# Further rows' products of an expert in three groups instead of six, with two transpositions and some conversions moved

## The chip, the cores and the metric

One core of a Trainium2 chip runs the whole kernel. The metric is the device time of one execution in microseconds, the median of several runs. TensorE multiplies, VectorE and ScalarE work on what it leaves in PSUM and on data in SBUF, GpSimd (POOL) gathers and scatters rows, SyncE (SP) issues most loads.

## What is computed

A hybrid encoder layer over 1024 positions of width 1024: a mixer (short convolution and a Fourier group), cross-attention to 256 memory tokens, and a mixture of experts. All that the change touches is in the last part:

```python
logits = (hf @ w_router).astype(jnp.float32) + b_router.astype(jnp.float32)
top_v, top_i = lax.top_k(logits, TOP_K)          # 4 of 32 experts for each position
...
gu = xb @ w_gate_up[e] + b_gate_up[e]
gate = jnp.minimum(gu[:, :D_EXPERT], SWIGLU_LIMIT)
up = jnp.clip(gu[:, D_EXPERT:], -SWIGLU_LIMIT, SWIGLU_LIMIT)
glu = gate * jax.nn.sigmoid(SWIGLU_ALPHA * gate)
return ((up + 1.0) * glu) @ w_down[e] + b_down[e]
```

Each expert has 1024 x 2048 weights for gate and up, and 1024 x 1024 for down, all fp32.

## The kernel before

**Records and chunks.** An expert works on a block of 128 gathered rows, its main rows. Experts with more rows than that get a second, smaller set, the further rows (rem in the code): 32 records for the 17 best-filled experts after the first one, 64 for the first (STATIC), none for the other 14. Experts stand in an order in which those with further rows (heavy) and those without (light) mostly alternate; expert 8 is heavy, between two light ones. An expert's weights are twelve chunks of 1 MB: 0 to 7 are gate and up (0 to 3 give the first half of the hidden width, g0 and u0, 4 to 7 the second, g1 and u1), 8 to 11 are down.

**Main products.** Weights and rows are split into a high part and a rest, so that three products in the faster fp32r form (`eh`, `el` of a chunk with the high part and the rest of the rows; lines 1072 to 1074) stand for one in fp32. `main_mm` issues twelve products a chunk. The split of a chunk, here called its conversion, is a ScalarE copy (`eh<-raw`, line 135) and a VectorE subtraction (`el<-raw,eh`, line 136).

**Further products.** `rem_mm` (line 1095) multiplies the further rows by the raw chunk in plain fp32. With 32 records a product needs 32 columns of the array, and four products (two halves of the contraction, two chunks) run side by side in four column strips. One call takes two chunks, eight products; six calls serve an expert. The sums of two calls share a bank: r0 (chunks 0 to 3), r1 (4 to 7), rd (8 to 11). The trace books each of these products twice, so eight show as x16. `take_rem` copies a bank out on ScalarE (`re<-r`, line 1113), `h_rem` transposes it, adds the bias and does its SwiGLU; `y_rem` finishes rd.

**Places.** The code writes its own order (manual schedule): each engine runs its instructions as they are written. An expert has 24 places, two a chunk: place 2j is in the middle of chunk j's products, 2j + 1 behind them. `PLACE_...` give the places of four transpositions for each kind of expert: the two halves of hh, the main rows' SwiGLU result (`h_main`: transposed on TensorE, line 1019, then split on both engines as `hthl`), and two for the next expert's rows (`x_main`, `xthl`). SwiGLU itself (`swiglu`, lines 1011 to 1014) is emitted at places 7 and 15, on VectorE and with one sigmoid on ScalarE. `REM` gives, in `plan`, the places of the further rows' steps relative to the expert: `lead` for the products, `lx` for `x_rem` (the further rows' own transposition, line 1045).

**Room.** Raw chunks and converted pairs live in one set of 18 slots. `load_more` issues a load, and `split_to` a conversion, at each place as far as a table (`AHEAD_...`) allows and there is room; a raw chunk's slot is free when its conversion and, in a heavy expert, the further product that reads it are written (`used_raw`). So when further products are written later, later conversions and loads follow.

Of the kernel before, what the change touches and what calls it, by code (L numbers as in the profile page):

```python
# [47 lines left out]
AHEAD_REM = (2, 3, 4, 5)  # L48
AHEAD_LOOP = (1, 5, 5, 6, 5, 5, 4, 5, 5, 7, 6, 7, 6, 4, 3, 6, 5, 6, 5, 6, 4, 5, 6, 5)
AHEAD_LAST = (1, 4, 3, 5, 4, 4, 3, 2, 2, 5, 4, 5, 4, 4, 3, 4, 3, 4, 3, 5, 4, 5, 4, 5)  # L50
REM = (2, 4, 0, 4, 4, 1)
PLACE_HEAVY = (13, 17, 19, 21)
PLACE_LIGHT = (13, 18, 20, 21)
PLACE_FIRST = (10, 17, 18, 21)
PLACE_LOOP = (13, 17, 21, 23)
PLACE_LAST = (11, 16, 0, 0)
KINDS = ("first", "heavy", "light", "loop", "last")
AHEAD = dict(zip(KINDS, (AHEAD_FIRST, AHEAD_HEAVY, AHEAD_LIGHT, AHEAD_LOOP, AHEAD_LAST)))
PLACE = dict(zip(KINDS, (PLACE_FIRST, PLACE_HEAVY, PLACE_LIGHT, PLACE_LOOP, PLACE_LAST)))

# [20 lines left out]
def kernel(ctx: ExitStack, tc: tile.TileContext, A, out, dbg=None):  # L81
    nc = tc.nc
# [10 lines left out]
    def mm_bank(name="mm"):  # L93
        return mmp.tile([P, H2], F32, name=name, tag="mm")

    def tp_bank(name="tp"):
        return tpp.tile([P, H2], F32, name=name, tag="tp")

    def sm_bank(name="sm"):
        return smp.tile([P, H2], F32, name=name, tag="sm")  # L100
# [4 lines left out]
    def s4(name, shape, dt=F32):  # L105
        return mp.tile(list(shape), dt, name=name, tag="s4", bufs=7)

    def t2(name, shape=(P, H2), dt=F32):
        return mp.tile(list(shape), dt, name=name, tag="t2", bufs=6)
# [8 lines left out]
    def f(ap):  # L118
        return ap.bitcast(F32)
# [459 lines left out]
    ps = {}  # L579
# [39 lines left out]
    for ft in range(KT):  # L619
        wh, wl = next_w(0)  # L620
        for h in range(2):
            xr = t2("xres")
            nc.sync.dma_start(out=xr, in_=A["xT"][h, ft])
            for g, (yh, yl) in enumerate(((ych, ycl), (yfh, yfl))):
                ps = mm_bank()
# [15 lines left out]
            q = t2("sq") if ft else row4[h]  # L641
# [102 lines left out]
    for fc in range(2):  # L744
        VW.append([(s8(f"vwh{fc}{q}", [P, 4, H2], F32R), s8(f"vwl{fc}{q}", [P, 4, H2], F32R)) for q in range(2)])
        for hd in range(4):
            w = next_w(0)
            for mt in range(2):
                ps = mm_bank()
# [3 lines left out]
                j = hd * 2 + mt  # L753
# [169 lines left out]
    ch = {}  # L923
# [18 lines left out]
    def scatter_add(dst, idx, src):  # L942
        nc.gpsimd.indirect_dma_start(out=dst, out_offset=bass.IndirectOffsetOnAxis(ap=idx, axis=0),  # L943
                                     in_=src, in_offset=None, compute_op=ALU.add)
# [35 lines left out]
    def whole(q):  # L980

        return q < WHOLE_FIRST or q >= NE * 12 - WHOLE_LAST

    def used_raw(q):
        ch[q][3] -= 1
        dead[0] += ch[q][3] == 0

    def split_to(n):
        while nsplit[0] < min(n, nload[0]):
            q = nsplit[0]  # L990
            c = ch[q]
            if not whole(q):
                if room() < 2:
                    return
                pairs[0] += 1
                c[1], c[2] = s8("eh", [P, 4, H2], F32R), s8("el", [P, 4, H2], F32R)
                split(c[0], c[1], c[2])
                used_raw(q)
            nsplit[0] += 1
# [9 lines left out]
    def swiglu(dst, g, u1, sg, u):  # L1009

        nc.scalar.activation(sg, g, AF.Sigmoid, scale=ALPHA)  # L1011
        nc.vector.tensor_scalar(u, u1, LIMIT + 1.0, 1.0 - LIMIT, op0=ALU.min, op1=ALU.max)
        nc.vector.scalar_tensor_tensor(u, sg, SIGMOID_LIMIT, u, op0=ALU.min, op1=ALU.mult)  # L1013
        nc.vector.scalar_tensor_tensor(dst, g, LIMIT, u, op0=ALU.min, op1=ALU.mult)  # L1014
# [62 lines left out]
            if k == 1 and middle:  # L1077
                middle()

    def rem_mm(i, j):  # L1080

        s = st[i]
        m = s["m"]
        c, g = (j // 4, (j % 4) // 2) if j < 8 else (0, (j - 8) // 2)
        lhs = s["xr"] if j < 8 else s["hr"]
        key = "r" + (str(c) if j < 8 else "d")
        n = 64 // m
        if g == 0:
            s[key] = sm_bank(key)
        ps = s[key]  # L1090
        for k in range(4 // n):
            for u in range(n):
                for t in range(2):
                    kk, o = u * 2 + k, (u * 2 + t) * m
                    nc.tensor.matmul(ps[o:o + m], lhs[:, g * 4 + kk, :], ch[12 * i + j - 1 + t][0][:, kk, :],  # L1095
                                     start=k == 0 and g == 0, stop=k == 4 // n - 1 and g == 1)
        for q in (j - 1, j):
            used_raw(12 * i + q)

    def glu_main(i, c):  # L1100
        s = st[i]
        s[f"h{c}"] = t2("hh")
        swiglu(s[f"h{c}"], s[f"g{c}"], s[f"u{c}"], t2("sg"), t2("u"))
# [7 lines left out]
    def take_rem(i, c):  # L1111
        r = st[i][f"re{c}"] = t2("re")
        nc.scalar.activation(r, st[i][f"r{c}"], AF.Copy)

    def h_rem(i, c):

        s = st[i]
        m = s["m"]
        if c == 0:
            s["hr"] = s4("hrt", [P, KT, m])  # L1120
        tb = tp_bank()
        for j in range(4):
            nc.tensor.transpose(tb[:, j * P:(j + 1) * P], s[f"re{c}"][:, j * P:(j + 1) * P], ident)
        tv = s[f"re{c}"][:, :8 * m].rearrange("p (j t n) -> p j t n", j=4, t=2)
        tw = tb.rearrange("p (j u t n) -> p j u t n", j=4, u=64 // m, t=2)
        nc.vector.tensor_tensor(tv, tw[:, :, 0], s["bT"][:, c, :, :, None].to_broadcast([P, 4, 2, m]), op=ALU.add)
        if m == 32:
            nc.vector.tensor_tensor(tv, tv, tw[:, :, 1], op=ALU.add)  # L1128
        ab = t2("ga").rearrange("p (a j n) -> p a j n", a=2, j=4)
        a, b = ab[:, 0, :, :m], ab[:, 1, :, :m]  # L1130
        swiglu(s["hr"][:, c * 4:c * 4 + 4, :], tv[:, :, 0], tv[:, :, 1], a, b)
# [8 lines left out]
    def y_rem(i):  # L1140
        s = st[i]
        m, rd = s["m"], s["rd"]
        n = 2 * m
        yr, w = t2("yr"), f(s["idr"][:n, 1:2])
        if m == 32:
            nc.scalar.activation(yr[:n], rd[n:], AF.Copy)
            nc.vector.tensor_tensor(yr[:n], rd[:n], yr[:n], op=ALU.add)
            nc.scalar.activation(yr[:n], yr[:n], AF.Copy, scale=w)
        else:
            nc.scalar.activation(yr, rd, AF.Copy, scale=w)  # L1150
        scatter_add(acc_d.rearrange("r (b w) -> (r b) w", w=H2), s["ids"][:n], yr[:n])

    def expert(i, hook=None, last=False):

        s = st[i]
        m, postponed = s["m"], s["r"] == STATIC
        n = i + 1 if i + 1 < NE else None
        kind = "first" if i == 0 else "last" if i == NE - 1 else "loop" if i == NE - 2 else "heavy" if m else "light"
        h0, h1, x0, x1 = PLACE[kind]
        ahead = AHEAD[kind]  # L1160
        todo = {p: [] for p in range(24)}
        todo[7].append(lambda: glu_main(i, 0))
        todo[15].append(lambda: glu_main(i, 1))

        def rem_postponed():
            x_rem(i)
            for p in (1, 3, 5, 7):
                rem_mm(i, p)
                if p % 4 == 3:
                    take_rem(i, p // 4)  # L1170
                load_more(eng=nc.gpsimd)
                split_to(12 * i + 7 + AHEAD_REM[p // 2])
            h_rem(i, 0)

        todo[h0].append(lambda: h_main(i, 0))
        todo[h1].append(lambda: h_main(i, 1))
        if n:
            todo[x0].append(lambda: x_main(n, 0))
            todo[x1].append(lambda: x_main(n, 1))
        if postponed:  # L1180
            todo[15].append(rem_postponed)
            todo[19] += [lambda: rem_mm(i, 9), lambda: h_rem(i, 1)]
            todo[23] += [lambda: rem_mm(i, 11), lambda: y_rem(i)]

        def place(p):
            for t in todo[p] + agenda.pop(24 * i + p, []):
                t()
            if p == 23 and not last:
                y_main(i)
            load_more(eng=nc.gpsimd if i == 0 else nc.sync)  # L1190
            split_to(12 * i + p // 2 + ahead[p])

        for j in range(12):
            load_more(eng=nc.gpsimd if i == 0 else nc.sync)
            if hook and j in hook:
                hook[j]()
            q = 12 * i + j
            main_mm(i, (0, 1, 2, 3, 4, 5, 6, 7, 8, 10, 9, 11)[j] if last else j, lambda: place(2 * j))
            if whole(q):
                used_raw(q)  # L1200
            else:
                pairs[0] -= 1
            place(2 * j + 1)

    def plan(i):

        lead, lx, lt, l0, l1, ly = REM
        at = lambda p, fn, *arg: agenda.setdefault(p, []).append(lambda: fn(*arg))
        p = 24 * i - 2 * lead + 1
        at(p + 2 - lx, x_rem, i)  # L1210
        for j in range(1, 12, 2):
            at(p + 2 * j, rem_mm, i, j)
        for c, l in ((0, l0), (1, l1)):
            at(p + 8 * c + 6 + lt, take_rem, i, c)
            at(p + 8 * c + 6 + l, h_rem, i, c)
        at(p + 22 + ly, y_rem, i)
# [309 lines left out]
    base, r = fin["base"], fin["r"]  # L1526
# [89 lines left out]
```

## Time and profile before

| | |
|---|---|
| median of 3 runs | 2056.21 us (2055.64 to 2057.71) |
| the profiled execution's own time | 2057.09 us |
| its span, first to last instruction | 2054.5 us |
| TensorE busy | 2014.3 us, 98% of the span |
| VectorE busy | 1546.7 us, 75% |
| ScalarE busy | 1117.8 us, 54% |
| main products of the experts (1072 to 1074) | 992 and 496 of each line, 390 to 415 ns booked for one |
| further products (1095) | x1152 r, 601 ns booked for one |

The experts begin near 600 us and fill the rest. Times of a product are booked durations; products overlap, so the distance from start to start is what counts for the end. Idle time of an engine stands in brackets, with what ended it.

### The profile page before, as it was taken

To read this page: it belongs to the slowest core of one execution; us is meant where nothing else is said; L and a number is where in the kernel's file an instruction comes from. 1 tells how busy PE (TensorE), PEld (TensorE's weight loads), DVE (VectorE), ACT (ScalarE), POOL (GpSimd) and SP (SyncE) were. 2 spreads that over 40 slices of the span, in tenths; PEclk is the share of its full clock that TensorE was granted. 3 is DMA by queue.
4 is the path that set the end of the run, shared out by engine and by line. 5 is a ranking of instruction groups with operands and counts; after the bars stand their busy time and mean duration, and the time that the engine had idled before them with its cause. 6 is when DMAs were issued, how large, how long until landed. Compare 5 with 4: busy or idle time off the path is not lost. (4 is left out here: it accounts for less than half of the span.)

```text
span 2054.5 us, 28594 instructions
## 1 busy us (share of the span) xinstructions
PE 2014.3 (98%) x10745; PEld 1522.1 (74%) x10745; DVE 1546.7 (75%) x1914; ACT 1117.8 (54%) x1195; POOL 238.4 (12%) x190
## 2 busy tenths in 40 slices
PE   8999999999988999999999999999999999999997
PEld 6888988888983567677776677776777676776764
DVE  6667768446575677888878788878888778888776
ACT  5233533334222565676656576666766566666664
POOL 0000100000133011021111111111111110110111
PEclk9999999999999999999999999999999999999998
DMA  4122434112358689898897888898998798898986
GB/s 157 47 62 72 124 129 158 42 41 91 106 190 291 222 288 362 298 326 329 308 360 279 308 322 324 311 374 285 330 327 308 280 372 300 322 332 305 354 290 265
DMA packets 104638, 513.25 MB, mean 250 GB/s; under 512 B 21297, under 2 KB 25650, under 8 KB 55346
## 3 DMA queue, kind: packets, MB, share of 16 engines
q1 hardware_dynamic: 83600, 445.87, 57.6%
q0 software_dynamic: 14080, 48.54, 9.5%
q10 hardware_dynamic: 6818, 16.99, 2.4%
q8 instruction: 85, 1.39, 0.3%
q14 instruction: 55, 0.45, 0.1%
HBM read 473.41 MB, written 37.95 MB: 249 GB/s over the span
## 5 line engine op out<-in xcount | busy, mean ns | idle before, releaser
L136 DVE TENSOR_TENSOR el<-raw,eh 128x2048 fp32r<-128x2048 f32 x372 | 831.6, 2286 | 125.5 <-ACT eh L135 125.5
L135 ACT ACTIVATE eh<-raw 128x2048 fp32r<-128x2048 f32 x372 | 692.5, 1910 | 28.7 <-PE g L1074 23.9
L1072 PE MATMUL g<-eh,xthl 128*128 128x512 f32 x992 | 393.7, 397 | 0.0
L1074 PE MATMUL g<-eh,xthl 128*128 128x512 f32 x992 | 386.7, 390 | 2.1 <-issue 2.1
L1073 PE MATMUL g<-el,xthl 128*128 128x512 f32 x992 | 387.6, 391 | 0.0
L1072 PEld LDWEIGHTS g<-eh,xthl 128*128 128x128 f32 x992 | 186.2, 188 | 66.6 <-issue 27.7
L1074 PEld LDWEIGHTS g<-eh,xthl 128*128 128x128 f32 x992 | 186.3, 188 | 42.7 <-issue 2.6
L1073 PEld LDWEIGHTS g<-el,xthl 128*128 128x128 f32 x992 | 186.4, 188 | 37.2
L1072 PE MATMUL d<-eh,hthl 128*128 128x512 f32 x496 | 205.9, 415 | 0.0
L1074 PE MATMUL d<-eh,hthl 128*128 128x512 f32 x496 | 195.1, 393 | 0.0
L1073 PE MATMUL d<-el,hthl 128*128 128x512 f32 x496 | 194.0, 391 | 0.0
L1095 PE MATMUL r<-raw,xrt 128*32 128x512 f32 (+1 forms) x1152 | 146.5, 601 | 0.7 <-ACT xrt L1046 0.7
L135 ACT ACTIVATE hthl<-tp 128x512 fp32r<-128x512 f32 x62 | 37.1, 599 | 163.0 <-PE tp L1019 163.0
L943 POOL DMA_INDIRECT acc_d<-y,idx x31 | 75.3, 2431 | 387.3 <-ACT y L1137 292.7
L1072 PEld LDWEIGHTS d<-eh,hthl 128*128 128x128 f32 x496 | 93.2, 188 | 28.0 <-ACT xthl L135 10.9
L1011 ACT ACTIVATE ga<-re 128x128 f32<-128x128 f32 (+1 forms) x36 | 11.4, 316 | 186.6 <-DVE re L1128 180.1
L1074 PEld LDWEIGHTS d<-eh,hthl 128*128 128x128 f32 x496 | 93.1, 188 | 21.2
L1073 PEld LDWEIGHTS d<-el,hthl 128*128 128x128 f32 x496 | 93.6, 189 | 16.0
L146 PE MATMUL mm<-xh,wh 128*128 128x512 f32 x232 | 92.2, 397 | 5.9 <-ACT xh L138 5.9
L939 POOL DMA_INDIRECT xg<-h_d,idx x32 | 55.2, 1726 | 359.1 <-DMA idx<-tab_d 242.0
L148 PE MATMUL mm<-xh,wl 128*128 128x512 f32 x232 | 91.0, 392 | 0.5 <-DVE wl L136 0.5
L147 PE MATMUL mm<-xl,wh 128*128 128x512 f32 x232 | 91.0, 392 | 0.0
(378 smaller groups left out, 3256.2 us busy)
## 6 DMA issues: line engine op xcount, KB each, us to landing
raw<-in_w_exp SPq DMA_DIRECT2D x375, 1024.0 KB, 7.7
raw<-in_w_exp POOLq DMA_DIRECT2D x9, 1024.0 KB, 13.3
wraw<-in_w_in SPq DMA_DIRECT2D x15, 512.0 KB, 5.1
xraw<-in_xT SPq DMA_DIRECT2D x16, 256.0 KB, 6.1
wraw<-in_w_k SPq DMA_DIRECT2D x8, 512.0 KB, 3.6
wraw<-in_w_v SPq DMA_DIRECT2D x8, 512.0 KB, 3.6
wraw<-in_w_out SPq DMA_DIRECT2D x8, 512.0 KB, 3.9
xres<-in_xT SPq DMA_DIRECT2D x16, 256.0 KB, 2.7
```

The costliest lines, as they stand in the source:

```text
L135: nc.scalar.activation(dh, src, AF.Copy)
L136: nc.vector.tensor_tensor(dl, src, f(dh), op=ALU.subtract)
L146: nc.tensor.matmul(ps, lh, rh, start=start and i == 0, stop=False)
L147: nc.tensor.matmul(ps, lh, rl, start=False, stop=False)
L148: nc.tensor.matmul(ps, ll, rh, start=False, stop=stop and i == n - 1)
L939: nc.gpsimd.indirect_dma_start(out=dst[:m], out_offset=None, in_=src[:, :], in_offset=bass.IndirectOffsetOnAxis(ap=idx[:m, 0:1], axis=0))
L943: nc.gpsimd.indirect_dma_start(out=dst, out_offset=bass.IndirectOffsetOnAxis(ap=idx, axis=0), in_=src, in_offset=None, compute_op=ALU.add)
L1011: nc.scalar.activation(sg, g, AF.Sigmoid, scale=ALPHA)
L1072: nc.tensor.matmul(ps, l[:, 0, kk, :], wh[:, k, :], start=j >= 8 and g == 0 and k == 0, stop=False)
L1073: nc.tensor.matmul(ps, l[:, 0, kk, :], wl[:, k, :], start=False, stop=False)
L1074: nc.tensor.matmul(ps, l[:, 1, kk, :], wh[:, k, :], start=False, stop=g == 1 and k == 3)
L1095: nc.tensor.matmul(ps[o:o + m], lhs[:, g * 4 + kk, :], ch[12 * i + j - 1 + t][0][:, kk, :], start=k == 0 and g == 0, stop=k == 4 // n - 1 ...
```

## The change

Three edits. `rem_mm` takes a list of halves: by default it does both calls of a bank in one go, sixteen products, so r0, r1 and rd are each one group; `plan` calls it for j = 3, 7 and 11, where formerly the second call of each bank stood. The first expert (STATIC) keeps its calls one by one. `REM` moves `x_rem` four places, two chunks, later. `PLACE_HEAVY` and `PLACE_LOOP` move the transposition of hh's first half from place 13 to 12.

```diff
--- before.py
+++ after.py
@@ -48,11 +48,11 @@
 AHEAD_REM = (2, 3, 4, 5)
 AHEAD_LOOP = (1, 5, 5, 6, 5, 5, 4, 5, 5, 7, 6, 7, 6, 4, 3, 6, 5, 6, 5, 6, 4, 5, 6, 5)
 AHEAD_LAST = (1, 4, 3, 5, 4, 4, 3, 2, 2, 5, 4, 5, 4, 4, 3, 4, 3, 4, 3, 5, 4, 5, 4, 5)
-REM = (2, 4, 0, 4, 4, 1)
-PLACE_HEAVY = (13, 17, 19, 21)
+REM = (2, 0, 0, 4, 4, 1)
+PLACE_HEAVY = (12, 17, 19, 21)
 PLACE_LIGHT = (13, 18, 20, 21)
 PLACE_FIRST = (10, 17, 18, 21)
-PLACE_LOOP = (13, 17, 21, 23)
+PLACE_LOOP = (12, 17, 21, 23)
 PLACE_LAST = (11, 16, 0, 0)
 KINDS = ("first", "heavy", "light", "loop", "last")
 AHEAD = dict(zip(KINDS, (AHEAD_FIRST, AHEAD_HEAVY, AHEAD_LIGHT, AHEAD_LOOP, AHEAD_LAST)))
@@ -1077,25 +1077,27 @@
             if k == 1 and middle:
                 middle()
 
-    def rem_mm(i, j):
+    def rem_mm(i, j, gs=(0, 1)):
 
         s = st[i]
         m = s["m"]
-        c, g = (j // 4, (j % 4) // 2) if j < 8 else (0, (j - 8) // 2)
+        j -= j % 4
         lhs = s["xr"] if j < 8 else s["hr"]
-        key = "r" + (str(c) if j < 8 else "d")
+        key = "r" + (str(j // 4) if j < 8 else "d")
         n = 64 // m
-        if g == 0:
+        if 0 in gs:
             s[key] = sm_bank(key)
         ps = s[key]
-        for k in range(4 // n):
-            for u in range(n):
-                for t in range(2):
-                    kk, o = u * 2 + k, (u * 2 + t) * m
-                    nc.tensor.matmul(ps[o:o + m], lhs[:, g * 4 + kk, :], ch[12 * i + j - 1 + t][0][:, kk, :],
-                                     start=k == 0 and g == 0, stop=k == 4 // n - 1 and g == 1)
-        for q in (j - 1, j):
-            used_raw(12 * i + q)
+        for g in gs:
+            for k in range(4 // n):
+                for u in range(n):
+                    for t in range(2):
+                        kk, o = u * 2 + k, (u * 2 + t) * m
+                        nc.tensor.matmul(ps[o:o + m], lhs[:, g * 4 + kk, :], ch[12 * i + j + 2 * g + t][0][:, kk, :],
+                                         start=k == 0 and g == 0, stop=k == 4 // n - 1 and g == 1)
+        for g in gs:
+            for t in range(2):
+                used_raw(12 * i + j + 2 * g + t)
 
     def glu_main(i, c):
         s = st[i]
@@ -1165,7 +1167,7 @@
         def rem_postponed():
             x_rem(i)
             for p in (1, 3, 5, 7):
-                rem_mm(i, p)
+                rem_mm(i, p, (p % 4 // 2,))
                 if p % 4 == 3:
                     take_rem(i, p // 4)
                 load_more(eng=nc.gpsimd)
@@ -1179,8 +1181,8 @@
             todo[x1].append(lambda: x_main(n, 1))
         if postponed:
             todo[15].append(rem_postponed)
-            todo[19] += [lambda: rem_mm(i, 9), lambda: h_rem(i, 1)]
-            todo[23] += [lambda: rem_mm(i, 11), lambda: y_rem(i)]
+            todo[19] += [lambda: rem_mm(i, 9, (0,)), lambda: h_rem(i, 1)]
+            todo[23] += [lambda: rem_mm(i, 11, (1,)), lambda: y_rem(i)]
 
         def place(p):
             for t in todo[p] + agenda.pop(24 * i + p, []):
@@ -1208,7 +1210,7 @@
         at = lambda p, fn, *arg: agenda.setdefault(p, []).append(lambda: fn(*arg))
         p = 24 * i - 2 * lead + 1
         at(p + 2 - lx, x_rem, i)
-        for j in range(1, 12, 2):
+        for j in (3, 7, 11):
             at(p + 2 * j, rem_mm, i, j)
         for c, l in ((0, l0), (1, l1)):
             at(p + 8 * c + 6 + lt, take_rem, i, c)
```

What this does to the order of each engine, in expert 8. On ScalarE from chunk 8's conversion to the second half's hthl, first before, then changed; `re<-r1` copies out the further products of chunks 4 to 7, the `eh` rows convert chunks 8, 9, 10 (ahead of `re`) and 11:

```order
L135 ACTIVATE eh_8844<-raw_8769 128x2048
L135 ACTIVATE eh_8860<-raw_8771 128x2048
L135 ACTIVATE eh_8864<-raw_8830 128x2048
L1113 ACTIVATE re_8882<-r1_8808 128x512
L135 ACTIVATE eh_8907<-raw_8832 128x2048
L135 ACTIVATE hthl_8917<-tp_8918 128x512
L1011 ACTIVATE sg_8938<-g1_8834 128x512
L1011 ACTIVATE ga_8960<-re_8882 128x4x32
L135 ACTIVATE hthl_8917<-tp_8982 128x512
```

```order
L135 ACTIVATE eh_8831<-raw_8765 128x2048
L135 ACTIVATE eh_8847<-raw_8767 128x2048
L1115 ACTIVATE re_8874<-r1_8857 128x512
L135 ACTIVATE hthl_8903<-tp_8904 128x512
L135 ACTIVATE eh_8911<-raw_8876 128x2048
L135 ACTIVATE eh_8915<-raw_8878 128x2048
L1011 ACTIVATE sg_8938<-g1_8821 128x512
L1011 ACTIVATE ga_8951<-re_8874 128x4x32
L135 ACTIVATE hthl_8903<-tp_8969 128x512
```

The conversion of chunk 10 has moved behind `re<-r1`, and those of 10 and 11 stand behind `hthl`, the first half's split.

On VectorE in the same stretch, before and changed, from chunk 8's subtraction to the second half's SwiGLU steps (`u`, `hh`, on g1):

```order
L136 TENSOR_TENSOR el_8845<-raw_8769,eh_8844 128x2048
L136 TENSOR_TENSOR el_8861<-raw_8771,eh_8860 128x2048
L136 TENSOR_TENSOR el_8865<-raw_8830,eh_8864 128x2048
L136 TENSOR_TENSOR el_8908<-raw_8832,eh_8907 128x2048
L136 TENSOR_TENSOR hthl_8917<-tp_8918,hthl_8917 128x512
L1012 TENSOR_SCALAR u_8939<-g1_8836 128x512
L1013 SCALAR_TENSOR_TENSOR u_8939<-sg_8938,u_8939 128x512
L1014 SCALAR_TENSOR_TENSOR hh_8937<-g1_8834,u_8939 128x512
```

```order
L136 TENSOR_TENSOR el_8832<-raw_8765,eh_8831 128x2048
L136 TENSOR_TENSOR el_8848<-raw_8767,eh_8847 128x2048
L136 TENSOR_TENSOR hthl_8903<-tp_8904,hthl_8903 128x512
L136 TENSOR_TENSOR el_8912<-raw_8876,eh_8911 128x2048
L136 TENSOR_TENSOR el_8916<-raw_8878,eh_8915 128x2048
L1012 TENSOR_SCALAR u_8939<-g1_8823 128x512
L1013 SCALAR_TENSOR_TENSOR u_8939<-sg_8938,u_8939 128x512
L1014 SCALAR_TENSOR_TENSOR hh_8937<-g1_8821,u_8939 128x512
```

Two subtractions now stand between `hthl` and the steps on g1.

On TensorE at place 15, where chunk 7's products (g) end and chunk 8's (d) begin, before and changed:

```order
L1072 MATMUL g_8836<-eh,xthl 128x512
L1073 MATMUL g_8836<-el,xthl 128x512
L1074 MATMUL g_8836<-eh,xthl 128x512
L1095 MATMUL rd<-raw,hrt 32x512 x8
L1123 MATMUL tp<-cst,re 128x128 x4
L1072 MATMUL d_8969<-eh,hthl 128x512
```

```order
L1072 MATMUL g_8823<-eh,xthl 128x512
L1073 MATMUL g_8823<-el,xthl 128x512
L1074 MATMUL g_8823<-eh,xthl 128x512
L1125 MATMUL tp<-cst,re 128x128 x4
L1072 MATMUL d_8956<-eh,hthl 128x512
```

The group of rd products has gone from here (all sixteen now stand at place 19); the transposition of re stays.

## Rows read from the trace of the kernel before

**Rows 1.** Page, part 1: busy us, share of the span, instructions, by engine
```profile
PE 2014.3 (98%) x10745; PEld 1522.1 (74%) x10745; DVE 1546.7 (75%) x1914; ACT 1117.8 (54%) x1195; POOL 238.4 (12%) x190
```

**Rows 2.** Waits, TensorE: line waited for, us in total, times, longest us
```profile
PE tp L1045 <- DMA xgr<-h_d,idr: 3.2, 1, 3.2
...
PE g L1074 <- issue: 2.1, 1, 2.1
```

**Rows 3.** Timeline, TensorE: start us, us, line, operation, tiles, forms, count, [idle before]
```profile
691.58 3.65 PE L1095 MATMUL rd<-raw,hrt 128*64 128x512 f32 x16
695.17 1.92 PE L1095 MATMUL r<-raw,xrt 128*32 128x512 f32 x16
...
697.60 0.39 PE L1072 MATMUL g<-eh,xthl 128*128 128x512 f32 x1
...
702.81 0.39 PE L1074 MATMUL g<-eh,xthl 128*128 128x512 f32 x1
```

**Rows 4.** Timeline, expert 8, r1 group to second transposition of hh: TensorE
```profile
1023.66 0.39 PE L1074 MATMUL g<-eh,xthl 128*128 128x512 f32 x1
1023.98 1.92 PE L1095 MATMUL r<-raw,xrt 128*32 128x512 f32 x16
1025.84 0.50 PE L1072 MATMUL g<-eh,xthl 128*128 128x512 f32 x1
...
1028.50 0.40 PE L1074 MATMUL g<-eh,xthl 128*128 128x512 f32 x1
1028.74 0.60 PE L1019 MATMUL tp<-cst,hh 128*128 128x128 f32 x4
1029.10 0.48 PE L1072 MATMUL g<-eh,xthl 128*128 128x512 f32 x1
...
1031.68 0.39 PE L1074 MATMUL g<-eh,xthl 128*128 128x512 f32 x1
...
1033.85 0.66 PE L1123 MATMUL tp<-cst,re 128*128 128x128 f32 x4
1034.26 0.48 PE L1072 MATMUL d<-eh,hthl 128*128 128x512 f32 x1
...
1037.10 0.60 PE L1019 MATMUL tp<-cst,hh 128*128 128x128 f32 x4
```

**Rows 5.** The same stretch: ScalarE (ACT) and VectorE (DVE)
```profile
1026.00 0.60 ACT L1113 ACTIVATE re<-r 128x512 f32<-128x512 f32 x1 [1.14 <-PE r L1095]
1026.49 1.91 ACT L135 ACTIVATE eh<-raw 128x2048 fp32r<-128x2048 f32 x1
...
1028.44 2.29 DVE L136 TENSOR_TENSOR el<-raw,eh 128x2048 fp32r<-128x2048 f32 x1 [0.46 <-ACT eh L135]
...
1029.44 0.60 ACT L135 ACTIVATE hthl<-tp 128x512 fp32r<-128x512 f32 x1 [1.03 <-PE tp L1019]
...
1030.65 0.68 DVE L136 TENSOR_TENSOR hthl<-tp,hthl 128x512 fp32r<-128x512 f32 x1
...
1032.10 0.69 DVE L1012 TENSOR_SCALAR u<-g 128x512 f32<-128x512 f32 x1 [0.77 <-PE g L1074]
...
1033.62 0.69 DVE L1014 SCALAR_TENSOR_TENSOR hh<-g,u 128x512 f32<-128x512 f32 x1
```

**Rows 6.** Timeline, last expert: a transposition that waits, and what stands behind it
```profile
2027.36 0.69 DVE L1014 SCALAR_TENSOR_TENSOR hh<-g,u 128x512 f32<-128x512 f32 x1
...
2028.20 0.63 PE L1019 MATMUL tp<-cst,hh 128*128 128x128 f32 x4 [1.51 <-DVE fr L1471]
...
2028.66 5.75 PE L1064 MATMUL d<-raw,hthl 128*128 128x512 f32 x13
```

**Rows 7.** Tile raw: the weight loads, from issue to landing
```profile
DMA to landing us min/median/max: 4.7/7.8/19.6
```

**Rows 8.** Windows: us, busy of each engine, granted clock, DMA share, GB/s
```profile
655.00:663.00 8.00, 6.16 (x26) 2.31 (x28) 0.49 (x4) 0.60 (x1) 0.00 (x0) 0.79 1.00 372
1959.00:1967.00 8.00, 5.87 (x35) 3.64 (x28) 4.60 (x3) 4.80 (x4) 0.00 (x0) 1.00 0.57 199
```

## The prediction, made before the changed kernel ran

> **What bounds the kernel now.** Read first the busy line [rows 1]: TensorE works in 98% of the span, and its list of waits adds up to some 28 us in 2054.5, almost all of it ahead of the first expert, in it and in the last; [rows 2] shows two that matter below. From expert to expert no wait on TensorE recurs. So its row of products sets the time, and a microsecond off it counts until something that it needs comes late. Busy time is no measure of a product: a plain one is booked at 0.39 us, but they start 0.2265 us apart (23 steps in 5.21 us, 697.60 to 702.81) [rows 3]. All prices below are from start to start.
>
> Then read one expert with further rows, number 8, round its first SwiGLU half's transposition, TensorE in [rows 4] and ScalarE and VectorE in [rows 5]. T is the start of the second group of r1 products (1023.98). Two things are to be seen: ScalarE waits 1.14 us for the group before it copies it out (1026.00) and 1.03 us for the transposition (1029.44); and VectorE is through with its weights just in time, since its first step on g1 waits 0.77 us for TensorE (1032.10).
>
> **What the change takes off TensorE.** In each of the 17 experts with 32 further records, six groups of eight products become three groups of sixteen; 51 changes into and out of such a group go. Alone, a group costs 1023.66 to 1025.84, 2.18 us, instead of one step of 0.23 [rows 4]. Its eight products are two rounds of four side by side. What two more rounds cost stands in [rows 3]: the 64-record group of eight is four rounds and takes 3.59 (691.58 to 695.17) where two take 1.86 (1023.98 to 1025.84), so 1.73. The change itself is then 2.18 - 0.23 - 1.73 = 0.22, and the products behind it are slow for a while: 11 steps in 2.66 us (1025.84 to 1028.50) instead of 2.49, 0.17 more. Together 0.39 a group, 1.17 an expert.
>
> Part of it comes back. Two transpositions of re stood right behind a group and now stand between main products. Behind a group one costs 0.41 (1033.85 to 1034.26) and its slow stretch takes the group's place; alone, as the one at 1028.74, it costs 0.37 (1028.50 to 1029.10 less a step) and 0.09 for the steps to 1031.68, so 0.13 more each. With 0.03 for the bias products, which get another neighbour, the gain is 1.17 - 0.26 - 0.03 = 0.88 an expert, 15.0 in all; in three experts that follow another one with further rows the further transpositions lose a place behind a group too, so I take **14.5 us**.
>
> The Trainium skill (TensorEngine Tiling (Array Packing), Tiling Modes, Key Properties) says that changing the tiling mode drains the engine. By that alone only entering and leaving the 32-column groups costs, the transpositions nothing, and the gain would be 17 x 1.17 = 19.9, the time 5.4 us lower than mine. The row at 1028.74 speaks against that last part: a transposition pays 0.46 without any narrow group beside it.
>
> **What the change moves.** *The further transpositions* come two chunks later, their products too, so they keep two chunks in hand. They now take the bank that VectorE frees with a subtraction (0.68, the row at 1030.65 [rows 5]): between 0 and 0.7 us for each, and I take 0, since there are two banks and that subtraction belongs to a transposition one to two chunks before. *Raw records* 0, 1, 4, 5, 8 and 9 are held two chunks longer, so loads of chunks 6, 7, 10 and 11 and of some in the next expert are issued later. The one that comes closest is chunk 11's: it is released at the end of chunk 4's products, a whole chunk (2.7 us) before T, and converted at T + 8. That is over 10 us for a transfer that takes 7.8 in the median [rows 7], but 19.6 at worst. I take 0; each microsecond of lateness there would count once in that expert.
>
> *The conversions.* A chunk is converted only when there is room, and room now comes later: the order shows chunk 10's conversion, which stood ahead of the copy of r1 on ScalarE, behind it and behind the hthl step, together with chunk 11's; VectorE's subtractions follow. This is where the time is decided, because both engines work in order and VectorE's second SwiGLU half stands behind those two subtractions. Step by step, all from [rows 4, 5]:
> - The r1 group has two rounds more. ScalarE copies it at T + 2.02 + 1.73 = T + 3.75 (it copied at 1026.00). Nothing useful stands ahead of it.
> - TensorE goes on at T + 1.86 + 1.73 = T + 3.59. The transposition of the first half now stands after 6 of the 12 products that took 2.90 (1025.84 to 1028.74): T + 5.04. ScalarE's hthl step begins 0.70 later (1028.74 to 1029.44): T + 5.74.
> - Only then chunk 10: its conversion 0.49 later (as 1026.00 to 1026.49), T + 6.23; VectorE's subtraction 1.95 after that (1026.49 to 1028.44), T + 8.18; chunk 11's follows at 2.21 (1028.44 to 1030.65), T + 10.39; the SwiGLU step on g1 at T + 12.60, though TensorE has had g1 ready since about T + 9.8 (1032.07 plus 1.73).
> - The half hh is done 2.21 later (1032.10 to 1033.62 plus 0.69): T + 14.81. A transposition that waits for VectorE starts 0.15 after it [rows 6]: T + 14.96.
> - TensorE arrives at that transposition earlier than before. It was there at T + 13.12 (1037.10), 2.8 us after hh was done (1034.31). Two rounds more for r1 give + 1.73; the rd group at 1031.99 has gone from this stretch: 1031.68 to 1034.26, 2.58, become one step and a transposition, 0.23 + 0.36, so - 1.99. It arrives at T + 12.86.
>
> So TensorE stands still for 14.96 - 12.86 = **2.1 us** in each such expert. Products that need nothing of it stand behind, but [rows 6] shows that they don't pass: there the engine waited 1.51 us for just such a transposition with d products of the first half behind it. All terms are counted from T, so whatever happens ahead of the r1 group doesn't alter it. Sixteen experts have this order; in the last one (expert 30) the conversions stand otherwise and I count half. 16.5 x 2.1 = 34.6 us. After the stall TensorE is later against ScalarE and VectorE than before, so the next expert's chunks have more in hand, and nothing else is late next.
>
> **The sum.** 34.6 - 14.5 = + 20.1. The profiled execution spans 2054.5 (its own time 2057.1, 0.9 above the median 2056.2); it becomes 2074.6, and the median **2076.3**, 1.0% slower.
>
> **Rivals.**
> 1. *Faster: the wait isn't there.* If chunk 10 and 11 are converted early enough that hh is done by T + 12.86, only the gain is left: 2056.2 - 14.5 = 2041.7. It turns at 2.1 us of ScalarE and VectorE work less ahead of hh. For it: before, there are 2.8 us to spare at this very place, and SwiGLU's first half is transposed half a chunk sooner, which is worth 1.45 us here. Against: the order puts both conversions behind that transposition, and two subtractions alone are 4.4 us. Chance 0.08.
> 2. *A wait of 0.6 to 1.1 us each:* gain and loss cancel (at 14.5 / 16.5 = 0.88), 2056. It needs the chain to be a microsecond shorter than each of its rows says. Chance 0.05.
> 3. *The standstill also costs clock.* In [rows 8] the granted clock averages 0.79 over 655 to 663, after TensorE had waited 3.2 us for its first further rows [rows 2]: 3.4 us of the stretch at 1.2 GHz, so 1.7 us of work lost. Once for each standstill, that is 28 us more, 2104. Against it: the wait of 2.1 us near 1963 [rows 2] left the clock at 1.00 [rows 8], and mine are as long as that one. Chance 0.04. The Trainium skill (TensorE: Matmul & The Clock Gate, Part 1) states that the engine is passed only half its clock pulses when it has been idle. By that rule this rival would have the larger share; the stretch round 1963 doesn't bear it out for a wait of this length.
> 4. *Late transfers on top:* if chunk 10 or 11 lands a microsecond or more after T + 6 as a rule, every expert pays that too: 16.5 a microsecond, 2092. Chance 0.03.
>
> **How the numbers follow.** My forecast has 0.80. Its own spread: a wait of 1.5 us gives 2066, one of 2.4 us 2081, and 0 to 0.3 us for the bank on top some 5 more. The range 2065 to 2086 holds nearly all of it; the rivals outside make up the rest. A measurement of this kernel can tell about 0.2% (4 us) from no change: faster by more 0.08 (rival 1), within it 0.05 (rival 2), slower by more 0.87.
>
> **What would show it.** Right: TensorE's list of waits has a new line, tp at the line of transpose_split waiting for VectorE (hh, or the steps behind it), some 16 times and near 2 us each; ScalarE waits longer for r1 and hthl; VectorE's step on g1 follows a subtraction without a gap; groups of 32 records in r and rd start 3.59 us before the next product. Wrong: that line is missing or under 0.9 us each (then it is rival 1 or 2), or the chain from r1 to hh is shorter than 14.8 us from T. A granted clock under 1.00 between 700 and 2000 us would be rival 3; a conversion that waits for a transfer, rival 4.

## The result and the profile after

The changed kernel takes **2091.4 us** in the median, the kernel before 2056.9 beside it: ratio 1.0169, 95% interval 1.0157 to 1.0181. The forecast was 2076.3 with a range of 2065 to 2086. The direction and the place of the loss are as forecast; 15 us come on top.

TensorE's list of waits has the line that the prediction asks for. First the head of the page (busy us, share of the span, instructions, by engine), beside [rows 1]:

```profile
PE 2017.6 (97%) x10745; PEld 1540.2 (74%) x10745; DVE 1543.1 (74%) x1914; ACT 1117.1 (53%) x1195; POOL 243.2 (12%) x190
```

Then the waits of TensorE (line waited for, us in total, times, longest us):

```profile
PE tp L1019 <- DVE hh L1014: 31.0, 16, 1.9
...
PE tp L1019 <- DVE fr L1473: 3.1, 1, 3.1
...
PE r L1096 <- DVEq L1414: 2.2, 1, 2.2
```

Sixteen times TensorE stands at the second half's transposition, for 1.94 us, where no such line stood before. Expert 8 again, as [rows 4, 5] show it before: the timeline from the r1 group (T = 1029.99) to that transposition, TensorE, then ScalarE, then VectorE:

```profile
1029.99 3.64 PE L1096 MATMUL r<-raw,xrt 128*32 128x512 f32 x32
...
1035.06 0.60 PE L1019 MATMUL tp<-cst,hh 128*128 128x128 f32 x4
...
1042.57 0.39 PE L1074 MATMUL d<-eh,hthl 128*128 128x512 f32 x1
1044.89 0.63 PE L1019 MATMUL tp<-cst,hh 128*128 128x128 f32 x4 [1.94 <-DVE hh L1014]
```

```profile
1033.69 0.60 ACT L1115 ACTIVATE re<-r 128x512 f32<-128x512 f32 x1 [0.99 <-PE r L1096]
1035.70 0.60 ACT L135 ACTIVATE hthl<-tp 128x512 fp32r<-128x512 f32 x1 [1.40 <-PE tp L1019]
1036.19 3.71 ACT L135 ACTIVATE eh<-raw 128x2048 fp32r<-128x2048 f32 x2
```

```profile
1036.33 0.69 DVE L136 TENSOR_TENSOR hthl<-tp,hthl 128x512 fp32r<-128x512 f32 x1 [0.89 <-ACT hthl L135]
1038.13 4.49 DVE L136 TENSOR_TENSOR el<-raw,eh 128x2048 fp32r<-128x2048 f32 x2 [1.11 <-ACT eh L135]
1042.54 0.68 DVE L1012 TENSOR_SCALAR u<-g 128x512 f32<-128x512 f32 x1
...
1044.06 0.69 DVE L1014 SCALAR_TENSOR_TENSOR hh<-g,u 128x512 f32<-128x512 f32 x1
```

The two conversions (`eh` x2, `el` x2) now stand between the first half's split and the SwiGLU steps, and `u` follows the second subtraction without a gap. Step by step, forecast and measured from T: copy of r1 3.75 and 3.70; first transposition 5.04 and 5.07; conversion of chunk 10 6.23 and 6.20; its subtraction 8.18 and 8.14; `u` 12.60 and 12.55; second transposition 14.96 and 14.90. TensorE arrives at 12.96 by the booked end of its last product and at 12.81 by the usual distance behind its start (1042.57 plus 0.23), which is how 12.86 was forecast; from there the wait is 2.09.

What the forecast did not count is in the granted clock. Two stretches of the same work, from the second transposition to the next one (x_main's), one in expert 8, one in expert 6; PEclk is the granted clock as a share of 2.4 GHz (columns: us, busy us and instructions of each engine, PEclk, DMA share, GB/s), with TensorE's whole stretch of repeating experts below them:

```profile
1044.89:1049.70 4.81, 4.81 (x16) 3.81 (x17) 3.46 (x7) 4.08 (x4) 0.00 (x0) 0.65 0.43 179
958.61:961.82 3.21, 3.21 (x17) 2.67 (x18) 2.01 (x6) 2.48 (x3) 0.00 (x0) 1.00 0.66 276
...
700.00:1985.00 1285.00, 1254.04 (x6545) 922.00 (x6544) 1029.69 (x862) 814.38 (x692) 175.49 (x91) 0.99 0.84 311
```

Both follow a wait of 1.94 us. After one the clock fell to 1.2 GHz for part of the stretch and the same work took 1.60 us longer; after the other it stayed at 2.4. Windows of 10 us round all sixteen waits show 0.83 eight times and 1.00 eight times. The number is not the same in every execution: the quickest of the four took 2088.4 us at a mean clock of 0.990, the longest 2093.8 at 0.987.

The same in whole experts, as starts of experts (first product on `g`). Changed kernel: expert 6 (a wait, full clock) takes 49.90, expert 8 (a wait, half clock behind it) 51.48, the light expert 9 36.30:

```profile
922.56 0.39 PE L1072 MATMUL g<-eh,xthl 128*128 128x512 f32 x1
...
972.46 0.39 PE L1072 MATMUL g<-eh,xthl 128*128 128x512 f32 x1
...
1008.85 0.39 PE L1072 MATMUL g<-eh,xthl 128*128 128x512 f32 x1
...
1060.33 0.39 PE L1072 MATMUL g<-eh,xthl 128*128 128x512 f32 x1
...
1096.63 0.39 PE L1072 MATMUL g<-eh,xthl 128*128 128x512 f32 x1
```

Kernel before, experts 8 and 9, 46.75 and 38.39:

```profile
1002.50 0.39 PE L1072 MATMUL g<-eh,xthl 128*128 128x512 f32 x1
...
1049.25 0.39 PE L1072 MATMUL g<-eh,xthl 128*128 128x512 f32 x1
...
1087.64 0.39 PE L1072 MATMUL g<-eh,xthl 128*128 128x512 f32 x1
```

A group of further products and the further transposition have moved from the light expert into the heavy one, so a pair has to be read together: 85.14 before, 86.2 after with a wait alone, 87.8 with half clock on top.

### The profile page after: what moved, and what is told of

The parts are those of the page before. It is cut to its first block, busy times and chain, and to the rows that moved or that the text cites. A ratio compares the mean times of both kernels' runs of the same rounds, so it can differ in the third digit from the quotient of the medians.

```text
span 2089.4 us, 28590 instructions
## 1 busy us (share of the span) xinstructions
PE 2017.6 (97%) x10745; PEld 1540.2 (74%) x10745; DVE 1543.1 (74%) x1914; ACT 1117.1 (53%) x1195; POOL 243.2 (12%) x190
## 5 line engine op out<-in xcount | busy, mean ns | idle before, releaser
L1072 PE MATMUL d<-eh,hthl 128*128 128x512 f32 x496 | 209.7, 423 | 0.0
L1074 PE MATMUL d<-eh,hthl 128*128 128x512 f32 x496 | 199.5, 402 | 0.7 <-DVE hthl L136 0.7
L1073 PE MATMUL d<-el,hthl 128*128 128x512 f32 x496 | 198.4, 400 | 0.0
L1096 PE MATMUL r<-raw,xrt 128*32 128x512 f32 (+1 forms) x1152 | 140.4, 600 | 2.8 <-DVEq L1414 2.2
L939 POOL DMA_INDIRECT xg<-h_d,idx x32 | 74.7, 2334 | 485.0 <-DMA idx<-tab_d 220.6
L1072 PEld LDWEIGHTS d<-eh,hthl 128*128 128x128 f32 x496 | 96.3, 194 | 31.1 <-issue 14.2
L1074 PEld LDWEIGHTS d<-eh,hthl 128*128 128x128 f32 x496 | 96.0, 194 | 23.4 <-DVE hthl L136 1.1
L943 POOL DMA_INDIRECT acc_d<-y,idx x31 | 68.3, 2203 | 343.4 <-ACT y L1139 300.8
L1096 PEld LDWEIGHTS r<-raw,xrt 128*32 128x32 f32 (+1 forms) x1152 | 36.6, 111 | 86.1 <-issue 83.9
```

What stands on the lines that cost most here:

```text
L939: nc.gpsimd.indirect_dma_start(out=dst[:m], out_offset=None, in_=src[:, :], in_offset=bass.IndirectOffsetOnAxis(ap=idx[:m, 0:1], axis=0))
L1072: nc.tensor.matmul(ps, l[:, 0, kk, :], wh[:, k, :], start=j >= 8 and g == 0 and k == 0, stop=False)
L1073: nc.tensor.matmul(ps, l[:, 0, kk, :], wl[:, k, :], start=False, stop=False)
L1074: nc.tensor.matmul(ps, l[:, 1, kk, :], wh[:, k, :], start=False, stop=g == 1 and k == 3)
```

## The experiments

Theory A: the late conversions of chunks 10 and 11 make hh late and TensorE waits; and the half clock is a consequence of that standstill. Rivals: B, the clock falls because sixteen narrow products run in a row, whatever waits; D, the sooner transposition alone does the harm; E, half clock belongs to certain experts, not to the wait. All kernels were timed beside the kernel before; the ratios are to that one. It took 2056.7 us beside the first four experiments and 2053.9 or 2053.1 beside the others, so for those go by the ratio and not by microseconds.

### Take the wait away, keep TensorE's order

```diff
-AHEAD_HEAVY = (..., 5, 6, 3, 3, 3, 3, 6, 1, ...)
+AHEAD_HEAVY = (..., 5, 5, 3, 3, 5, 3, 6, 1, ...)
```

> The changed kernel with one number of the table for heavy experts lowered and one raised, so that chunk 11 is converted behind the second half's SwiGLU instead of ahead of it; TensorE's order is the changed kernel's, word for word. Theory A (the 16 waits of 1.94 us come from the two subtractions ahead of hh, and the half clock comes from the standstill): hh is done at about T + 12.0 instead of T + 14.75, TensorE arrives at T + 12.96, the waits go (31.0 us), and with them the eight spells of half clock behind them (8 x 1.55 = 12.4 us): 2091.4 - 43.4 = 2048. Rival B (the clock falls because sixteen products run side by side in narrow strips, whatever waits): the waits go, the spells stay: 2060.

Measured: **2043.2 us, ratio 0.9929 (0.9913 to 0.9946)**; faster than both kernels, and 5 us below theory A's 2048. Expert 8 of this kernel, with T = 1016.62, TensorE and then VectorE, and its granted clock:

```profile
1016.62 3.64 PE L1096 MATMUL r<-raw,xrt 128*32 128x512 f32 x32
...
1029.43 0.60 PE L1019 MATMUL tp<-cst,hh 128*128 128x128 f32 x4
```

```profile
1024.76 2.29 DVE L136 TENSOR_TENSOR el<-raw,eh 128x2048 fp32r<-128x2048 f32 x1 [1.11 <-ACT eh L135]
1026.97 0.68 DVE L1012 TENSOR_SCALAR u<-g 128x512 f32<-128x512 f32 x1
...
1028.49 0.69 DVE L1014 SCALAR_TENSOR_TENSOR hh<-g,u 128x512 f32<-128x512 f32 x1
...
1032.21 2.29 DVE L136 TENSOR_TENSOR el<-raw,eh 128x2048 fp32r<-128x2048 f32 x1 [1.19 <-ACT eh L135]
```

```profile
700.00:1940.00 1240.00, 1240.00 (x6562) 915.12 (x6564) 1031.20 (x863) 811.94 (x693) 167.56 (x91) 1.00 0.88 323
```

One subtraction is left ahead of `u`, chunk 11's stands behind hh. `hh` begins at T + 11.87 instead of T + 14.07, the transposition has no wait behind its name, and both the waits and the half clock are gone between 700 and 1940. TensorE is busy in the whole stretch. This kernel gives the price list: experts 8 and 9 take 47.75 and 36.30,

```profile
995.48 0.39 PE L1072 MATMUL g<-eh,xthl 128*128 128x512 f32 x1
...
1043.23 0.39 PE L1072 MATMUL g<-eh,xthl 128*128 128x512 f32 x1
...
1079.53 0.39 PE L1072 MATMUL g<-eh,xthl 128*128 128x512 f32 x1
```

so the regrouping is worth 85.14 - 84.05 = 1.09 us a pair, a wait of 1.94 costs 49.90 - 47.75 = 2.15 from start to start, and half clock behind it 51.48 - 49.90 = 1.58 (expert 6 takes 47.75 here too, so that 6 and 8 may be compared). With these prices theory A's figure would have been 2091.4 - 34.4 - 12.6 = 2044.4.

### Keep the wait, fill it with useless products

```diff
+        tb = None
+        if c and s["m"] == 32 and i < NE - 2:
+            tb, wh = tp_bank(), ch[12 * i + 9][1]
+            for j in range(8):
+                nc.tensor.matmul(tb, s["ht"][:, 0, j % 4, :], wh[:, j % 4, :], start=True, stop=True)
-        transpose_split(lambda j: ..., s["ht"], c, whole(12 * i + 8))
+        transpose_split(lambda j: ..., s["ht"], c, whole(12 * i + 8), tb)
```

`transpose_split` takes the bank that the useless products have written (`tb`) instead of a new one; that line of it is left out here.

> The changed kernel with eight useless products (128x512) ahead of the second half's transposition in the 16 heavy experts before the last; they write the bank which the transposition then overwrites. They last 8 x 0.2265 = 1.81 us, just short of the wait of 1.94, so hh and the transposition come when they came. Theory A (standstill costs clock): the time of the stretch stays or grows by up to 0.2 us an expert, and the eight spells of half clock go: 2091.4 - 12.4 = 2079, up to 2082; more work, less time. Rival B (the clock falls for the narrow strips): spells stay, 2091 to 2095.

Measured: **2077.5 us**, ratio 1.0096 (1.0079 to 1.0113): 14.0 us less than the changed kernel, with 128 more products. Expert 8 of this kernel on TensorE (the useless products are the row of line 1115), and below it the window of its repeating experts:

```profile
1037.89 0.39 PE L1074 MATMUL d<-eh,hthl 128*128 128x512 f32 x1
1038.12 1.97 PE L1115 MATMUL tp<-eh,hthl 128*128 128x512 f32 x8
1040.13 0.66 PE L1019 MATMUL tp<-cst,hh 128*128 128x128 f32 x4
```

```profile
700.00:1975.00 1275.00, 1274.48 (x6694) 938.01 (x6693) 1032.02 (x863) 815.53 (x693) 165.41 (x91) 1.00 0.86 314
```

The useful work stands still as long as before: 2.01 us from 1038.12 to the transposition, and the time above the first experiment's kernel, 34.2 us, is 16 x 2.14. Only the half clock is gone. Groups, conversions and transfers are the changed kernel's, so B falls: narrow groups alone don't lower the clock here, the standstill does. This run separates the two costs of one wait.

### Move the waiting transposition

Half a chunk later:

```diff
-PLACE_HEAVY = (12, 17, 19, 21)
+PLACE_HEAVY = (12, 18, 19, 21)
```

> The changed kernel with the second half's transposition half a chunk later in heavy experts (place 18 instead of 17); the conversions stay. TensorE arrives 6 products (1.36 us) later, so 0.58 us of each wait is left: 16 x 1.36 = 21.7 us less, 2069.7. Theory A adds: a standstill of 0.58 us is followed by half clock less often than one of 1.94, at best never: 2057 to 2070, mean clock above 0.989. Rival B: the eight spells stay, 2070, clock 0.989.

Measured: 2081.2 us, ratio 1.0113 (1.0096 to 1.0130). A miss: slower than either theory says. Waits of TensorE and clock between 700 and 1980:

```profile
PE d L1074 <- DVE hthl L136: 21.5, 16, 1.3
PE tp L1019 <- DVE hh L1014: 9.2, 16, 0.6
```

```profile
700.00:1980.00 1280.00, 1249.26 (x6567) 913.52 (x6569) 1032.55 (x864) 816.28 (x694) 180.72 (x91) 1.00 0.86 313
```

The wait at the transposition shrank to 0.58 as expected, but a product on d that needs the split of this transposition now waits 1.34. The expectation had forgotten this next user. Together that is as long as the 1.94 that it was to relieve, yet the clock stays at 1.00: 32 waits of up to 1.34 us, none with half clock.

Half a chunk sooner:

```diff
-PLACE_HEAVY = (12, 17, 19, 21)
+PLACE_HEAVY = (12, 16, 19, 21)
```

> The changed kernel with the second half's transposition half a chunk sooner still (place 16): TensorE arrives 1.36 us earlier, each of the 16 waits is 3.3 us instead of 1.94. Theory A: half clock follows more often than 8 of 16 times, nearly every time: 2091.4 + 21.7 + up to 8 x 1.55 = 2118 to 2126, mean clock 0.982 or so. Rival E (the eight experts with half clock are fixed by something else in them, not by the wait): 2113, mean clock 0.989.

Measured: 2121.9 us, ratio 1.0336 (1.0320 to 1.0352). Its waits, and three of the sixteen windows of 10 us round them:

```profile
PE tp L1019 <- DVE hh L1014: 53.3, 16, 3.7
```

```profile
780.00:790.00 10.00, 8.80 (x46) 6.03 (x50) 8.28 (x11) 5.00 (x5) 0.00 (x0) 0.83 0.51 179
...
1047.00:1057.00 10.00, 8.08 (x30) 6.49 (x34) 8.38 (x11) 4.59 (x5) 0.00 (x0) 0.66 0.45 165
...
1191.00:1201.00 10.00, 8.02 (x54) 5.12 (x58) 8.51 (x12) 5.00 (x5) 0.00 (x0) 1.00 0.51 174
```

Thirteen windows are like the first, two like the second, one like the third: half clock at 15 of 16 waits of 3.31 us (one of them 3.67); in some it begins up to 0.9 us before the wait ends. E falls.

### The same standstill without the regrouping

The kernel before, its second transposition at place 15 in heavy experts:

```diff
-PLACE_HEAVY = (13, 17, 19, 21)
+PLACE_HEAVY = (13, 15, 19, 21)
```

> The kernel before, six groups of eight, with the second half's transposition at place 15 instead of 17 in heavy experts, where it has to wait for hh: from rows 4 and 5 hh is done at 1034.31 and TensorE would be there at 1031.91, so it waits 2.55 us in 16 experts: 2056.2 + 41 = 2097 by the waits alone. Theory A: half clock follows at least as often as behind 1.94 us, 8 to 16 times at 1.55: 2109 to 2122, mean clock under 0.99. Rival B: no wide groups of sixteen, so clock as before, 2097.

Measured: 2116.7 us, ratio 1.0291 (1.0273 to 1.0308). Its waits, and two of the windows round them:

```profile
PE tp L1019 <- DVE hh L1014: 38.7, 16, 2.8
```

```profile
959.00:969.00 10.00, 8.18 (x41) 4.86 (x42) 4.29 (x10) 3.15 (x4) 0.00 (x0) 0.83 0.56 218
...
1048.00:1058.00 10.00, 7.91 (x46) 5.47 (x47) 5.84 (x10) 4.43 (x4) 0.00 (x0) 1.00 0.70 254
```

Eleven windows of sixteen show 0.83, and the time lies in theory A's range. Six groups of eight don't protect: between 700 and 1960 the kernel before has a clock of 1.00 and no wait, and with waits it loses clock too.

### Undo and do the moves one by one

The changed kernel with the first transposition back at place 13:

```diff
-PLACE_HEAVY = (12, 17, 19, 21)
+PLACE_HEAVY = (13, 17, 19, 21)
-PLACE_LOOP = (12, 17, 21, 23)
+PLACE_LOOP = (13, 17, 21, 23)
```

> The changed kernel with the first half's transposition back at place 13, three groups of sixteen kept. Theory A: conversions 10 and 11 are still late (room), but now stand ahead of the first half's split: hthl's subtraction ends at T + 11.3 by the steps of the prediction, a d product of chunk 8 waits for it about 1 us instead of the transposition waiting 1.94, hh is done at T + 13.5 when TensorE arrives after T + 13.9. 16 waits of about 1 us, hardly any half clock: 2091.4 - 34.7 - 12.4 + 16 = 2060. Rival D (the sooner transposition made the loss): no wait at all, 2043 to 2046.

Measured: 2053.4 us, ratio 0.9996 (0.9987 to 1.0006), the same as before. TensorE's waits between 700 and 1950, and VectorE in expert 8, where T is 1017.07:

```profile
PE d L1074 <- DVE hthl L136: 10.5, 16, 0.7
```

```profile
1023.24 4.50 DVE L136 TENSOR_TENSOR el<-raw,eh 128x2048 fp32r<-128x2048 f32 x2 [1.45 <-ACT eh L135]
1027.65 0.69 DVE L136 TENSOR_TENSOR hthl<-tp,hthl 128x512 fp32r<-128x512 f32 x1
1028.25 0.68 DVE L1012 TENSOR_SCALAR u<-g 128x512 f32<-128x512 f32 x1
```

The conversions are still behind the r1 group, but ahead of the split instead of behind it. Their subtractions begin at T + 6.2 instead of T + 8.1, so `u` comes at T + 11.2 instead of T + 12.55; the split comes late instead, at T + 10.6, and a d product waits 0.66 us for it. No half clock follows. That is theory A's wait in theory A's place, 0.66 long instead of about 1; the rival's "no wait at all" is wrong, yet the sooner transposition turned a draw into a loss.

The kernel before with only that transposition moved (the same two lines the other way round):

```diff
-PLACE_HEAVY = (13, 17, 19, 21)
+PLACE_HEAVY = (12, 17, 19, 21)
-PLACE_LOOP = (13, 17, 21, 23)
+PLACE_LOOP = (12, 17, 21, 23)
```

> The kernel before with one part of the change alone: the first half's transposition half a chunk sooner (place 12) in heavy experts and in expert 30; groups and the further rows' transposition as before. Theory A (that move does harm only when the conversions of chunks 10 and 11 stand behind it): here they stand ahead of it as before, no new wait, same time as before, within 2 us. Rival D (the move itself makes hh late): waits tp <- DVE hh, 5 us or more slower.

Measured: 2054.2 us, ratio 1.0000 (0.9990 to 1.0009), and no wait of TensorE between 700 and 1950. Behind that comes one wait that the kernel before has too, at the same product: the 2.1 us in expert 30 where the code jumps past a loop over more blocks of rows, which has none to do here. There it left the clock at 1.00 [rows 2, 8]; here half clock follows:

```profile
1958.89 0.50 PE L1074 MATMUL g<-eh,xthl 128*128 128x512 f32 x1 [2.13 <-issue]
```

```profile
1955.00:1965.00 10.00, 7.87 (x34) 5.30 (x27) 5.23 (x3) 4.79 (x4) 0.00 (x0) 0.83 0.67 261
```

The first experiment's kernel with it moved back:

```diff
 AHEAD_HEAVY = (..., 5, 5, 3, 3, 5, 3, 6, 1, ...)
-PLACE_HEAVY = (12, 17, 19, 21)
+PLACE_HEAVY = (13, 17, 19, 21)
-PLACE_LOOP = (12, 17, 21, 23)
+PLACE_LOOP = (13, 17, 21, 23)
```

> The kernel of e1_conv_later (chunk 11 converted behind the second half's SwiGLU) with the first half's transposition back at place 13. Theory A (what counts is how many subtractions stand ahead of hh, not where that transposition is): hthl's subtraction ends at about T + 9.1, before the d products want it, no wait in either place: as e1_conv_later, ratio to before 0.993 +- 0.002. Rival D (its place alone decides): a wait on d of about 0.66 us is left as in e7_h0_back, 16 x 0.95 = 15 us more, ratio 1.000.

Measured: 2041.0 us, ratio 0.9931 (0.9915 to 0.9948), no wait either. So the place of the first transposition does nothing by itself; it does harm only together with the late conversions.

Both moves on the kernel before:

```diff
-REM = (2, 4, 0, 4, 4, 1)
+REM = (2, 0, 0, 4, 4, 1)
-PLACE_HEAVY = (13, 17, 19, 21)
+PLACE_HEAVY = (12, 17, 19, 21)
-PLACE_LOOP = (13, 17, 21, 23)
+PLACE_LOOP = (12, 17, 21, 23)
```

> The kernel before with the two moves alone: the further rows' transposition two chunks later, the first half's transposition half a chunk sooner in heavy experts and in expert 30; six groups of eight as before. Theory A: raw records are freed where they were, no conversion moves, no wait is new, and nothing is gained: 2056 (2054 to 2058). Rival D (the sooner transposition is itself what makes hh late): a line tp <- DVE hh some 16 times, up to 2 us each, 2056 to 2090.

Measured: 2073.0 us, ratio 1.0097 (1.0082 to 1.0113): far outside theory A's range, and inside rival D's by another cause than D's. TensorE's waits between 700 and 1965:

```profile
PE r L1095 <- ACT xrt L1046: 16.3, 16, 3.4
```

There is no wait for hh, which again speaks against D. But with six groups the first r group stands right behind the further transposition in its new place and waits for ScalarE's copy of it: 0.47 us as a rule, 3.39 in three experts, and the clock falls after these three. The edit was badly chosen: the further transposition can only move later because the regrouping moves its first products too.

### The last two experts

The first experiment's kernel loses time in experts 30 and 31: 4.4 and 2.3 us more than in the kernel before. An attempt to get it back:

```diff
-BEYOND = 1
+BEYOND = 2
-AHEAD_LOOP = (..., 7, 6, 7, 6, 4, ...)
+AHEAD_LOOP = (..., 7, 5, 5, 5, 4, ...)
-PLACE_LAST = (11, 16, 0, 0)
+PLACE_LAST = (13, 16, 0, 0)
```

> The kernel of e1_conv_later with its last two experts repaired: expert 30 converts chunks 10 and 11 behind the first half's split (two numbers of its table), the jump past the empty loop comes one chunk later, so that its wait of 2.15 us falls into main products instead of into the r group, and the last expert's first transposition of hh stands one chunk later. Theory A (waits, and half clock behind some of them): the d wait of 0.66 us in expert 30 goes, the 2.90 us wait for fr in the last expert becomes 0.2 us or less, and with it the half clock at both places: 0.9 + 2.7 + 2.65 + 1.6 us less, 2043.2 - 7.9 = 2035.4. Rival: the wait of the last expert only moves on to the next product that needs the same work, 2039 to 2042.

Measured: 2039.3 us, ratio 0.9931 (0.9917 to 0.9944): no better than 0.9929. Of the waits in question, the one on d in expert 30 is 0.33 us instead of 0.66, and there are left

```profile
PE tp L1019 <- DVE fr L1473: 2.3, 1, 2.3
...
PE tp L1125 <- SPq L1414: 2.1, 1, 2.1
```

The expectation named the wrong transposition: the one that waits in the last expert is the second half's, 28.5 us into it, not the first's. Why it is late there was not tried. The half clock is gone in the last expert, but still follows the jump.

## Why the prediction was right in direction and wrong in size

**What bounds the kernel, and the chain: right.** Every step from T to the second transposition is within 0.1 us of its term, and the wait is 2.09 for 2.1, counted as in the forecast from start to start. The list shows 1.94, because it counts from the booked end of the last product, 0.39 us after its start, where the next one would have started after 0.23. A whole expert pays 2.15, and 16 x 2.15 = 34.4 against 34.6 in the sum. Taking one subtraction out of the chain takes the wait away, as rival 1's condition says (it turns at 2.1 us of work ahead of hh).

**The gain: nearly right, made of misses both ways.** The regrouping is worth 1.09 us rather than 0.88 in a heavy expert that follows a light one, and 0.7 to 0.8 in the three that follow a heavy one. In experts 2 to 29 that is 15.7 us: in the first experiment's kernel they run from 743.18 to 1933.48, in the kernel before from 746.92 to 1952.91. Ahead of them 2.8 is gained, where the prediction had one expert's share: 0.7 in expert 1, and 2.1 in expert 0, which the first group of expert 1 has left (73.7 us in two other kernels with six groups, 71.6 in all with three). The 78.61 us of expert 0 in the profile of the kernel before are no measure: they hold the wait of 3.2 us for a transfer with half clock behind it [rows 2, 8], which no other kernel here shows. Experts 30 and 31 lose 6.7, where the prediction counted half a wait; 1.0 of it is the group that has moved from expert 29 into 30, and in each of the two the first experiment's kernel has a spell of half clock, the kernel before none. By these rows about 12 us are left, by the medians 13.5 (2056.7 less 2043.2), for 14.5. By the sentence of the Trainium skill (TensorEngine Tiling (Array Packing), Tiling Modes, Key Properties) the prediction made the regrouping worth 1.17 an expert with transpositions costing nothing; 1.09 lies nearer to that than to 0.88, but no run here measures the parts by themselves.

**The step that failed is rival 3, "the standstill also costs clock", given 0.04 and left out of the sum.** The rows that spoke for it were in the prediction, with the price: 1.7 us, measured 1.58. It was dismissed because one wait of 2.13 us, the one near 1963, left the clock at 1.00 [rows 2, 8]. One instance was taken for a rule: behind that same wait half clock follows in 8 of the 12 kernels, the changed one among them. Sixteen equal waits in the changed kernel fell out eight to eight. Counted by the runs, with the profiled execution of each kernel:

| wait of TensorE | half clock follows |
|---|---|
| 0.47 to 0.66 us (three kernels) | 0 of 45 |
| 1.34 us | 0 of 16 |
| 1.94 us (changed kernel) | 8 of 16 |
| 2.09 to 2.23 us (the jump past the loop in expert 30, all twelve kernels) | 8 of 12 |
| 2.40 us, one of 2.76 (kernel before, made to wait) | 11 of 16 |
| 3.31 to 3.67 us (two kernels) | 18 of 19 |

Eight times 1.58 is 12.6 us. The sum with what the runs measured: 34.4 for standing still, 12.6 for the clock, less 13.5: 33.5; the difference of the medians is 34.5, and the rest lies inside the spread of the runs (2088.4 to 2093.8). The filled kernel, 14.0 us faster than the changed one, measures the clock's part directly and comes near to 12.6.

The Trainium skill (TensorE: Matmul & The Clock Gate, Part 1) says that idling takes the engine to half its pulses; this case's runs agree, and they show besides that waits of one and the same length can go either way.

**Rival 4 (late transfers): not seen.** In expert 8 the conversions of chunks 10 and 11 begin where ScalarE comes free, at 1036.19 right behind hthl, and all conversions between 700 and 1985 together waited 2.4 us for transfers.

**Open:** which of several equal waits are hit. The runs were read for how often, not for which. The jump shows it best: the same wait of 2.13 us at the same product left the clock at 1.00 in the kernel before and was followed by half clock when only the first transposition was moved.

## What to carry to other kernels

When an engine that must never stop gets a new wait, price it twice: its length, and the chance of half clock behind it times what one such spell costs; a single wait that went unpunished is no evidence about the next sixteen. Where a change frees buffers later, list what is converted or copied late because of it, and look what stands behind that in the same engine's order: here one conversion put behind the urgent step, by two numbers of a table, turned 1.7% slower into 0.7% faster. If a wait can't be avoided, compare it with the kernel that fills it with useless work: the difference is the clock's part.

## What the runs showed of the hardware that was not expected

- Useless work made the kernel faster: 128 more products of 128x512, 14.0 us less.
- Two waits of 0.58 and 1.34 us some 8 us apart cost no clock in 16 experts, one of 1.94 us did in 8 of 16.
- A wait costs more than the list of waits shows: one of 1.94 us costs 2.15 from start to start, one of 0.66 costs 0.92 (experts of 48.71 us, against 47.79 in the kernel with chunk 11 converted later and the first transposition at the same place). For the longer one, 0.15 of the 0.21 is the list's way of counting, from the booked end of the product before.
